# A two-layer decoder trunk: expert steps merged in pairs, their products chained in program order, and the last scale spread by rounded products

## The chip, the cores and the metric

The kernel runs on one core of one Trainium2 chip. The metric is the device time of one execution in microseconds; of before three runs are given, and their median counts. A profile is one further execution, taken by the hardware profiler.

## The reference, cut to what matters

The input is 256 tokens of 1024 values in float32. Two layers follow a first layer norm; each has a token mixer (two attention branches, not touched by this change apart from its first products) and a channel mixer: a dense SwiGLU in layer 0, and in layer 1 eight experts of which each token takes two.

```python
def moe_swiglu(x, w_router, w_gate_up, w_down):
    logits = (x @ w_router).astype(jnp.float32)
    top_v, top_i = lax.top_k(logits, TOP_K)
    gates = jax.nn.softmax(top_v, axis=-1)
    combine = jnp.sum(jax.nn.one_hot(top_i, N_EXPERTS, dtype=jnp.float32) * gates[..., None], axis=-2)
    y = jnp.zeros_like(x)
    for e in range(N_EXPERTS):
        y = y + combine[..., e:e + 1].astype(x.dtype) * swiglu(x, w_gate_up[e], w_down[e])
    return y

    # each sub-layer, in reference():
    h = layer_norm(DEEPNORM_ALPHA * h + f, ln_ffn_g[l], ln_ffn_b[l])
```

An expert has a gate-and-up matrix of 1024 x 7168 and a down matrix of 3584 x 1024, all float32: eight of them are 352 MB, and every one is read, whatever the router says.

## The kernel before, in words

The work stands in program order: first layer norm, mixer of layer 0, `out_norm` (residual and layer norm), the dense channel mixer, `out_norm`, mixer of layer 1, `out_norm` with the router beside it, and then the experts, which end in the last layer norm. A scheduler orders each engine's instructions by their priority (program order, apart from the parts under `high_priority`) and by dependencies that the kernel adds by hand. TensorE, VectorE (DVE), ScalarE (ACT) and the queue of DMA issues (SP) each work off their own list in order: an instruction that waits holds up all behind it on its engine.

**The experts.** The experts are put into eight places by how many tokens they have. Places 0, 1 and 2 form the *big* chain, places 7, 6, 5, 4 and 3 the *small* one. Each chain is a Python generator that gives one step at a time.

- A step of the big chain loads one piece of 1024 KB or less into a `raw` buffer (`slot`, L389). ACT makes its upper part `whi` (L433) and DVE the rest `wlo` (L434), in halves of 128x1024, and `tile_mm` multiplies them: eight products with the rounded tokens (`whi,xh` and `whi,xl`, alternating) and four `wlo,xh`, called *rounded products* below; they go to TensorE at L304. At place 0 a third set of tokens rides along, `far`: its products read the raw piece itself (`mm<-raw,xs`, 64 columns). They are collected in `beside` and issued for two steps together (`together`, called by `step`).
- A step of the small chain loads two pieces (768 KB in the up part, 1024 KB in the down part) and multiplies the raw float32 values with packed tokens (`aux<-raw,xs` in the up part, `aux<-raw,eh` in the down part; no split).

Both chains draw their `raw` buffers from one ring of eight (`RING`); a buffer comes free when the last instruction that reads it is done, and the next load into it waits on SP for that. The pieces of the first eight small steps are loaded ahead, seven of them in the ring and nine in a second pool (`AHEAD`, L382), and the ring also takes one piece of the ninth step ahead of its turn. The eight small steps go first. Then `both_chains` opens the pool for `whi` and calls `merge`, which takes one step of one chain or the other so that both get through the parts of `MERGE` in proportion:

```python
while i < ex or j < ey:
    if i < ex and (i - at[0]) * (ly - at[1]) <= (j - at[1]) * (ex - at[0]):
        i += 1
        yield next(x)
    else:
        j += 1
        yield next(y)
```

Inside a step, `in_turn` chains the products of a Packed tile one behind the other; those of `tile_mm` are not chained and not tied to what stands before or behind them. `later_on` puts a small function off to the end of a later step (`flush`): transposes, sums, and the spread below.

**The last scale.** `spread_rows` (called at step 160) loads the gain and the bias of the last layer norm, 1024 values each, as four rows of 512 (L1620) and spreads each over 128 partitions: one float32 product with a row of ones into a `tp` bank (two buffers), and a copy by ACT (L1613), all four in one put-off function.

**The first half.** `keep_busy` (L306) issues products of ones whose result nobody reads (`o<-onesb`). `out_norm` issues three of them at its end, for both tiles of 128 tokens alike, then the scale and the shift of tile 0 and of tile 1 (`ln_scale`: small DVE steps L491 and L495; L546: the shift with gain and bias), and after each tile its transposes (L469). The silu of the dense mixer is on ACT (L1071), with a product on DVE (L1072 before, L1075 after the change).

Of the kernel before, what the change touches and what calls it, by code (L numbers as in the profile page):

```python
# [9 lines left out]
F32R = mybir.dt.float32r  # L10
# [69 lines left out]
class Packed:  # L80
# [138 lines left out]
    def last(self, keys, ws, st):  # L219
# [9 lines left out]
        def products(x, ks, w, first, last):  # L229
            out = []  # L230
            for i, (r, _, j) in enumerate(ks):
                out += self.times([(x[half[i % 2]], 512 * i, 512)], self.hid[r, j], w, first and i < 2, last and i >= len(ks) - 2)
            b.in_turn(out, [w.load])

# [35 lines left out]
class Body:  # L270
# [463 lines left out]
    def mixer(self, l, xT):  # L734
# [7 lines left out]
        for i, k0 in enumerate((0, 2, 4, 6)):  # L742
            wpc = self.piece(w[:, k0:k0 + 2, C_FV:C_FV + 520], self.hold if i else self.first)
            for t in range(2):
                for hf in range(2):
                    if i == 0:
                        vps[t, hf] = self.aux_bank() if hf else self.mm_bank()
                    self.tok(vps[t, hf][:, :260], xT, k0, wpc, t, hf * 260, hf * 260 + 260, i == 0, i == 3)
        if l == 0:
            with tc.issue_after(self.made.ins):  # L750
                self.setup_bias()
# [158 lines left out]
        for i in range(2):  # L910
            wpc = [self.piece(wb[j][:, :, 512 * i:512 * i + 512]) for j in range(2)]
            for jp in range(2):
                parts = []
# [40 lines left out]
    def out_norm(self, h, xT, w, nk, g, b, routed=False):  # L954
# [26 lines left out]

        def norm(t):
            if t == 0:
                out.extend(self.stream("hT"))
            return self.ln_apply(r[t], self.ln_scale(st[t]), gb,
                                 lambda hf: self.put_T([out[0][p, hf] for p in "hl"], r[t][:, hf * 512:(hf + 1) * 512], t))
# [29 lines left out]
        with self.tc.manual_schedule(engines={mybir.EngineType.PE}):  # L1016
            for i in range(3):
                load(*p[i])
                go(*p[i], 0, 0)
                go(*p[i], 0, 1)  # L1020
            load(*p[3])
            for n, (i, part, t) in enumerate(((0, 0, 1), (0, 1, 1), (1, 0, 1), (3, 0, 0), (3, 1, 0), (1, 1, 1), (2, 0, 1), (2, 1, 1), (3, 0, 1), (3, 1, 1))):
                go(*p[i], t, part)
                for f, *x in behind.get(n, ()):
                    if routed and n == 9:
                        self.keep_busy(3, spare)
                    f(*x)
            self.keep_busy(11 if routed else 3, spare)
        if routed:
# [15 lines left out]
        with self.tc.high_priority():  # L1045
            self.hold = norm(0)
        self.first, self.late = None, self.hold
        norm(1)
        return r, out[1]

# [218 lines left out]
    def tile_mm(self, outs, x, w, flats, first, last):  # L1269

        for n, out in enumerate(outs):
            for i, act in enumerate(x):
                for j, part in ((0, "h"), (1, "h")):
                    self.mm(out, act[j], w.at(part, flats[i] + n * 512, 512), first and i + j == 0, False)
        for n, out in enumerate(outs):
            for i, act in enumerate(x):
                self.mm(out, act[0], w.at("l", flats[i] + n * 512, 512), False, last and i == len(x) - 1)

    def together(self, products=(), loads=()):

        products, loads = list(products), list(loads)
        for p, l in self.beside:
            products += p
            loads += l
        self.beside = []
        if products:
            self.in_turn(products, loads)

# [6 lines left out]
    def in_turn(self, products, after=()):  # L1295
# [7 lines left out]
        for x, y in zip(made, made[1:]):  # L1303
            self.behind(y, x, mybir.DependencyClass.NoSync)

    def behind(self, ins, other, kind):
# [167 lines left out]
    def moe(self, ctx, h, routing, g, b):  # L1474
# [19 lines left out]
        eidi = next(routing)  # L1494
        self.put_off, self.nrows = [], 5
        acc = []
# [31 lines left out]
        def merge(x, y, parts, lead):  # L1528
# [4 lines left out]
            for n, (ex, ey) in enumerate(ends):  # L1533
                ly = ey - (lead if n == len(ends) - 1 else 0)
                while i < ex or j < ey:
                    if i < ex and (i - at[0]) * (ly - at[1]) <= (j - at[1]) * (ex - at[0]):
                        i += 1
                        yield next(x)
                    else:
                        j += 1  # L1540
                        yield next(y)
                at = ex, ey
# [12 lines left out]
        for n, z in enumerate(both_chains()):  # L1555
# [17 lines left out]
            if n == 160:  # L1573
                gb = self.spread_rows(g, b)
            if n == 14:
# [23 lines left out]
    def spread_rows(self, g, b):  # L1599

        nc = self.nc
        one = self.wk.tile([1, 128], F32, name="one_row", bufs=1)
        nc.gpsimd.memset(one, 1.0)
        gb = [[self.pp.tile([128, 512], F32, name="ln_gb", tag="far", bufs=4) for _ in range(2)] for _ in range(2)]
        for row, xs in zip((g, b), gb):
            for hf, x in enumerate(xs):
                nc.sync.dma_start(x[0:1], row[None, hf * 512:(hf + 1) * 512])

        def f():
            for x in gb[0] + gb[1]:  # L1610
                bk = self.tp_bank()
                self.mm(bk, one, x[0:1], True, True)
                nc.scalar.activation(x, bk, AF.Copy)  # L1613
        self.later_on(f)
        return gb

# [155 lines left out]
```

## Time and profile before

| | us |
|---|---|
| median of three runs | 1463.91 (1463.39 to 1464.29) |
| the profiled execution | 1463.79 |
| its span in the profile | 1462.1 |
| TensorE busy | 1399.9 (96%) |
| DVE busy | 812.4 (56%) |
| ACT busy | 655.4 (45%) |

The busy time of TensorE (PE) is modelled to the end of a product, waits inside a pipelined row among it, so that 96% does not mean that it works at its peak; PEld is the weight load that runs beside it. The page cuts the span into 40 slices and gives for each the busy tenths of an engine, the TensorE clock that was granted (PEclk) and the share of the 16 DMA engines. The row DMA and the row GB/s are the ones to read beside the engines: 453.42 MB are moved, 310 GB/s over the span. An engine in square brackets in a timeline row is what ended its idle time.

### The profile page before, as it was taken

The page shows a single profiled execution, that of the slowest core. Times are in us where ns is not written, and L with a number is a line of the kernel's source. Part 1 is how long each engine was busy: PE and PEld are TensorE (multiplying, and loading weights), DVE is VectorE, ACT ScalarE, POOL GpSimd, SP SyncE. Part 2 cuts the span into 40 slices and gives each one's busy share as a digit, 9 for nine tenths or more (in the row PEclk, how much of TensorE's full clock was granted, in tenths as well). Part 3 has the DMA queues.
Part 4 walks back from the last instruction along what each step waited for, and adds up shares of the span by engine and source line. Part 5 has one row for each costly group of instructions (what it writes and reads, how often), then busy time and mean ns, then how long its engine had stood idle before and what let it go on. Part 6 is the DMA issues. An engine that isn't in the chain of part 4 may idle for free. (4 is left out here: it accounts for less than half of the span.)

```text
span 1462.1 us, 20101 instructions
## 1 busy us (share of the span) xinstructions
PE 1399.9 (96%) x7581; PEld 929.2 (64%) x7581; DVE 812.4 (56%) x1233; ACT 655.4 (45%) x954; POOL 16.9 (1%) x44
## 2 busy tenths in 40 slices
PE   8999999999999999999999999999999999999985
PEld 6878978888788789755444453467675455445531
DVE  7757786665577676624253443377667245344423
ACT  4656546664266663133433332356555233323310
POOL 4000000000000000000000000000000000000000
PEclk9999999999999999999999999999999899999998
DMA  9633546555384347699999999999999899999994
GB/s 297 220 120 135 181 146 205 198 167 207 106 265 151 115 145 300 253 385 407 405 418 415 415 419 422 420 419 418 418 420 420 331 421 409 421 420 420 419 366 189
DMA packets 135767, 453.42 MB, mean 310 GB/s; under 512 B 8079, under 2 KB 63399, under 8 KB 108013
## 3 DMA queue, kind: packets, MB, share of 16 engines
q1 hardware_dynamic: 134872, 450.99, 79.5%
q0 software_dynamic: 784, 1.05, 0.4%
q8 instruction: 62, 1.02, 0.3%
q14 instruction: 45, 0.36, 0.1%
q10 hardware_dynamic: 4, 0.01, 0.0%
HBM read 450.96 MB, written 1.05 MB: 309 GB/s over the span
## 5 line engine op out<-in xcount | busy, mean ns | idle before, releaser
L434 DVE TENSOR_TENSOR wlo<-raw,whi 128x1024 fp32r<-128x1024 f32 (+2 forms) x456 | 516.6, 1161 | 414.7 <-ACT whi L433 402.5
L433 ACT ACTIVATE whi<-raw 128x1024 fp32r<-128x1024 f32 (+2 forms) x456 | 442.1, 1005 | 380.9 <-DMA raw<-in_w_expert_gate_up 140.4
L304 PE MATMUL mm<-hT,whi 128*128 128x512 f32 x672 | 234.8, 398 | 0.0
L304 PE MATMUL aux<-raw,xs 128*32 128x512 f32 (+3 forms) x1280 | 188.1, 552 | 4.3 <-DMA raw<-in_w_expert_gate_up 3.5
L304 PE MATMUL mm<-hT,wlo 128*128 128x256 f32 x672 | 175.8, 281 | 0.0
L304 PE MATMUL mm<-whi,xh 128*128 128x512 f32 x336 | 140.7, 419 | 4.7 <-ACT whi L433 3.4
L304 PEld LDWEIGHTS mm<-hT,whi 128*128 128x128 f32 x672 | 121.5, 188 | 23.8 <-issue 0.7
L304 PE MATMUL mm<-whi,xl 128*128 128x512 f32 x336 | 133.2, 396 | 0.0
L304 PEld LDWEIGHTS mm<-hT,wlo 128*128 128x128 f32 x672 | 126.8, 189 | 9.1 <-issue 2.0
L304 PEld LDWEIGHTS aux<-raw,xs 128*32 128x32 f32 (+1 forms) x1280 | 57.4, 121 | 108.6 <-issue 99.4
L304 PE MATMUL aux<-raw,eh 128*32 128x512 f32 (+1 forms) x560 | 93.0, 604 | 11.3 <-DMA raw<-in_w_expert_down 7.7
L304 PE MATMUL mm<-wlo,xh 128*128 128x512 f32 x336 | 98.7, 402 | 0.8 <-DVE wlo L434 0.7
L304 PEld LDWEIGHTS mm<-whi,xh 128*128 128x128 f32 x336 | 63.4, 189 | 56.6 <-issue 23.2
L304 PE MATMUL mm<-whi,eh 128*128 128x512 f32 x336 | 89.1, 405 | 5.6 <-ACT whi L433 5.6
L304 PEld LDWEIGHTS mm<-whi,eh 128*128 128x128 f32 x336 | 59.7, 188 | 36.7 <-ACT whi L433 18.6
L304 PEld LDWEIGHTS mm<-wlo,xh 128*128 128x128 f32 x336 | 62.2, 189 | 23.1 <-DVE wlo L434 4.6
L304 PEld LDWEIGHTS mm<-whi,xl 128*128 128x128 f32 x336 | 63.5, 189 | 11.7
L304 PEld LDWEIGHTS aux<-raw,eh 128*32 128x32 f32 (+1 forms) x560 | 26.2, 121 | 60.7 <-issue 58.2
L429 ACT ACTIVATE sums<-mm 128x512 f32<-128x512 f32 x84 | 50.2, 600 | 31.9 <-PE mm L304 30.5
L304 PE MATMUL aux<-hT,whi 128*128 128x512 f32 x160 | 56.2, 396 | 0.0
L304 PE MATMUL mm<-raw,xs 128*64 128x512 f32 x224 | 54.2, 605 | 0.0
L304 PE MATMUL mm<-whi,hT 128*128 128x260 f32 (+2 forms) x192 | 50.9, 335 | 1.2 <-DVE hT L434 0.9
(345 smaller groups left out, 1607.8 us busy)
## 6 DMA issues: line engine op xcount, KB each, us to landing
raw<-in_w_expert_gate_up SPq DMA_DIRECT2D x140, 1024.0 KB, 11.9
raw<-in_w_expert_down SPq DMA_DIRECT2D x111, 1024.0 KB, 12.7
raw<-in_w_expert_gate_up SPq DMA_DIRECT2D x112, 768.0 KB, 11.5
raw<-in_w_in SPq DMA_DIRECT2D x36, 1024.0 KB, 5.1
raw<-in_w_ffn_gate_up SPq DMA_DIRECT2D x22, 1024.0 KB, 5.1
raw<-in_w_ffn_down SPq DMA_DIRECT2D x10, 1024.0 KB, 4.9
raw<-in_w_out SPq DMA_DIRECT2D x8, 1024.0 KB, 5.0
raw<-in_w_in SPq DMA_DIRECT2D x8, 520.0 KB, 6.7
```

The lines of the kernel that those rows point to most:

```text
L304: self.made = self.nc.tensor.matmul(out, lhsT, rhs, start=start, stop=stop)
L429: self.nc.scalar.activation(x, bank, AF.Copy, scale=scale)
L433: return (self.nc.scalar.activation(hi, src, AF.Copy), self.nc.vector.tensor_sub(lo, src, hi.bitcast(F32)))
L434: self.nc.vector.tensor_sub(lo, src, hi.bitcast(F32)))
```

## The change

It has five parts.

1. `merge` takes two steps of a chain at a time.
2. `in_line` chains a group's products like `in_turn`, and also ties its first product behind the last one of the group before (`self.line`), for both chains: on TensorE all products of expert pieces stand in program order. In `tile_mm` the products are the same, in the same order.
3. `spread_rows` splits each of the four rows into two rounded parts and spreads it by two rounded one-row products and an ACT copy, one row every fourth step from step 164 on.
4. `keep_busy` gets nine products in place of three in the two out_norms that have no router, and eight are added in the first mixer, among the products of its values.
5. The scale of the second tile in `out_norm` is computed at the high priority of the first tile's norm.

```diff
@@ first mixer
+                if l == 0 and i == 2 and t == 0:
+                    self.keep_busy(8, self.o_bank(), self.made)
@@ out_norm
-        def norm(t):
+        def norm(t, scale):
...
-            return self.ln_apply(r[t], self.ln_scale(st[t]), gb,
+            return self.ln_apply(r[t], scale, gb,
...
-            self.keep_busy(11 if routed else 3, spare)
+            self.keep_busy(11 if routed else 9, spare)
...
-            self.hold = norm(0)
+            self.hold = norm(0, self.ln_scale(st[0]))
+            scale = self.ln_scale(st[1])
...
-        norm(1)
+        norm(1, scale)
@@ tile_mm, together and Packed.last
+        self.in_line(products)
...
-            self.in_turn(products, loads)
+            self.in_line(products, loads)
@@
+    def in_line(self, products, after=()):
+
+        made = self.in_turn(products, after)
+        if self.line:
+            self.behind(made[0], self.line, mybir.DependencyClass.NoSync)
+        self.line = made[-1]
@@ merge
-                        i += 1
-                        yield next(x)
+                        for _ in range(min(2, ex - i)):
+                            i += 1
+                            yield next(x)
                     else:
-                        j += 1
-                        yield next(y)
+                        for _ in range(min(2, ey - j)):
+                            j += 1
+                            yield next(y)
@@ experts
             if n == 160:
-                gb = self.spread_rows(g, b)
+                gb, spreads = self.spread_rows(g, b)
+            if n > 160 and n % 4 == 0 and spreads:
+                self.later_on(spreads.pop(0))
@@ spread_rows
+        oner = self.wk.tile([1, 128], F32R, name="one_row_r", bufs=1)
+        nc.vector.tensor_copy(oner, one)
...
-        def f():
-            for x in gb[0] + gb[1]:
-                bk = self.tp_bank()
-                self.mm(bk, one, x[0:1], True, True)
-                nc.scalar.activation(x, bk, AF.Copy)
-        self.later_on(f)
-        return gb
+                def f(x=x):
+                    parts = [self.row_tile("parts", F32R)[0:1] for _ in range(2)]
+                    self.split(*parts, x[0:1])
+
+                    def spread():
+                        bk = self.tp_bank()
+                        self.in_turn([(bk, oner, p, i == 0, i == 1) for i, p in enumerate(parts)])
+                        nc.scalar.activation(x, bk, AF.Copy)
+                    self.later_on(spread)
+                spreads.append(f)
+        return gb, spreads
```

Three places of the order follow. The first is TensorE (PE) behind the eighth small step, before the change: the next two small steps (`aux`; `raw_6073` is the piece loaded ahead) stand ahead of the transposes of the eighth step's rows and of the first big piece, `raw_6265`, whose far product stands among its rounded products.

```order
L304 MATMUL aux_6299<-raw_6073,xs_6075 32x384 x4
L304 MATMUL aux_6299<-raw_6297,xs_6075 32x384 x4
L304 MATMUL aux_6299<-raw_6312,xs_6075 32x384 x4
L304 MATMUL aux_6299<-raw_6314,xs_6075 32x384 x4
L148 MATMUL tp_6290<-ident_123,rows_6250 128x128 x4
L304 MATMUL mm_6275<-whi_6267,xh_6139 128x512
L304 MATMUL mm_6275<-whi_6267,xl_6140 128x512
L304 MATMUL mm_6276<-whi_6267,xh_6139 128x512
L304 MATMUL mm_6276<-whi_6267,xl_6140 128x512
L304 MATMUL mm_6289<-raw_6265,xs_6141 64x512 x4
```

After the change the transposes come first, then 24 rounded products of two big pieces (the last six of them are shown), then the far products of both, `raw_6286` and `raw_6318`, and then the small steps, from the piece loaded ahead (`raw_6094`) on.

```order
L304 MATMUL mm_6297<-whi_6324,xh_6160 128x512
L304 MATMUL mm_6297<-whi_6324,xl_6161 128x512
L304 MATMUL mm_6296<-wlo_6321,xh_6160 128x512
L304 MATMUL mm_6296<-wlo_6325,xh_6160 128x512
L304 MATMUL mm_6297<-wlo_6321,xh_6160 128x512
L304 MATMUL mm_6297<-wlo_6325,xh_6160 128x512
L304 MATMUL mm_6310<-raw_6286,xs_6162 64x512 x4
L304 MATMUL mm_6310<-raw_6318,xs_6162 64x512 x4
L304 MATMUL aux_6350<-raw_6094,xs_6096 32x384 x4
L304 MATMUL aux_6350<-raw_6348,xs_6096 32x384 x4
L304 MATMUL aux_6350<-raw_6359,xs_6096 32x384 x4
```

So the two small steps have moved behind two big ones, and the far product that reads `raw_6286` last behind all rounded products of both.

The second place is SP's list of loads at the same place, with what each waits for. Before, the first big piece is followed by small ones and big ones in turn:

```order
L389 DMA raw_6265<-in_w_expert_gate_up 128x2x1024 [waits DMAHW7_49,PE_49]
L389 DMA raw_6297<-in_w_expert_gate_up 128x1536 [waits DMAHW0_49,PE_49]
L389 DMA raw_6312<-in_w_expert_gate_up 128x1536 [waits DMAHW1_49,PE_49]
L389 DMA raw_6314<-in_w_expert_gate_up 128x1536 [waits DMAHW2_49,PE_49]
L389 ISA
L389 DMA raw_6324<-in_w_expert_gate_up 128x2x1024 [waits DMAHW3_49,PE_49]
L389 DMA raw_6346<-in_w_expert_gate_up 128x1536 [waits DMAHW4_49,PE_49]
```

After it, two big pieces come first, then seven small ones, of which the sixth (`raw_6383`) is the first to wait for the buffer of the big piece `raw_6286`, which DVE and TensorE read:

```order
L389 DMA raw_6286<-in_w_expert_gate_up 128x2x1024 [waits DMAHW7_49,PE_49]
L389 ISA
L389 DMA raw_6318<-in_w_expert_gate_up 128x2x1024 [waits DMAHW0_49,PE_49]
L389 DMA raw_6348<-in_w_expert_gate_up 128x1536 [waits DMAHW1_49,PE_49]
L389 DMA raw_6359<-in_w_expert_gate_up 128x1536 [waits DMAHW2_49,PE_49]
L389 DMA raw_6361<-in_w_expert_gate_up 128x1536 [waits DMAHW3_49,PE_49]
L389 DMA raw_6371<-in_w_expert_gate_up 128x1536 [waits DMAHW4_49,PE_49]
L389 DMA raw_6373<-in_w_expert_gate_up 128x1536 [waits DMAHW5_49,PE_49]
L389 DMA raw_6383<-in_w_expert_gate_up 128x1536 [waits DMAHW6_49,DMAHW7_49,DVE_49,PE_49]
```

The second big piece is loaded before the small ones now, and the eighth load of the list has become dependent on TensorE's first far product.

The third place is DVE in the first `out_norm`, at the scale of the second tile. Before, the steps of the scale (L491, L495) and the shift (L546) stand ahead of the dense mixer's product with the silu:

```order
L495 SCALAR_TENSOR_TENSOR rs_y_2210<-rs_q_2211,rs_y_2210 128x1
L491 SCALAR_TENSOR_TENSOR rs_q_2211<-rs_y_2210,rs_m_2212 128x1
L495 SCALAR_TENSOR_TENSOR rs_y_2210<-rs_q_2211,rs_y_2210 128x1
L546 SCALAR_TENSOR_TENSOR h_2013<-h_2013,rs_y_2210,ln_gb_2008 128x512
L546 SCALAR_TENSOR_TENSOR h_2013<-h_2013,rs_y_2210,ln_gb_2010 128x512
L1072 TENSOR_TENSOR silu_2310<-silu_2310,mm_2261 128x256
```

After it, that product stands ahead of the last step of the scale:

```order
L495 SCALAR_TENSOR_TENSOR rs_y_2225<-rs_q_2226,rs_y_2225 128x1
L491 SCALAR_TENSOR_TENSOR rs_q_2226<-rs_y_2225,rs_m_2227 128x1
L1075 TENSOR_TENSOR silu_2325<-silu_2325,mm_2276 128x256
L495 SCALAR_TENSOR_TENSOR rs_y_2225<-rs_q_2226,rs_y_2225 128x1
L546 SCALAR_TENSOR_TENSOR h_2022<-h_2022,rs_y_2225,ln_gb_2017 128x512
L546 SCALAR_TENSOR_TENSOR h_2022<-h_2022,rs_y_2225,ln_gb_2019 128x512
```

The product of the silu has moved up by three rows, and the two L546 behind it.

More of the change, by code (lines that the diff above doesn't have):

```diff
@@ L232, in products @@
                 out += self.times([(x[half[i % 2]], 512 * i, 512)], self.hid[r, j], w, first and i < 2, last and i >= len(ks) - 2)
-            b.in_turn(out, [w.load])
+            b.in_line(out, [w.load])
         def give(h, t, y):
@@ L1269, in tile_mm @@
     def tile_mm(self, outs, x, w, flats, first, last):
+        products = []
         for n, out in enumerate(outs):
             for i, act in enumerate(x):
-                for j, part in ((0, "h"), (1, "h")):
-                    self.mm(out, act[j], w.at(part, flats[i] + n * 512, 512), first and i + j == 0, False)
+                for part in act:
+                    products.append((out, part, w.at("h", flats[i] + n * 512, 512), first and i == 0 and part is act[0], False))
         for n, out in enumerate(outs):
             for i, act in enumerate(x):
-                self.mm(out, act[0], w.at("l", flats[i] + n * 512, 512), False, last and i == len(x) - 1)
+                products.append((out, act[0], w.at("l", flats[i] + n * 512, 512), False, last and i == len(x) - 1))
+        self.in_line(products)
     def together(self, products=(), loads=()):
@@ L1304, in in_turn @@
             self.behind(y, x, mybir.DependencyClass.NoSync)
+        return made
+    def in_line(self, products, after=()):
[3 more added lines that the diff above has]
+        self.line = made[-1]
     def behind(self, ins, other, kind):
@@ L1494, in moe @@
         eidi = next(routing)
-        self.put_off, self.nrows = [], 5
+        self.put_off, self.nrows, self.line = [], 5, None
         acc = []
@@ L1603, in spread_rows @@
         nc.gpsimd.memset(one, 1.0)
+        oner = self.wk.tile([1, 128], F32R, name="one_row_r", bufs=1)
+        nc.vector.tensor_copy(oner, one)
         gb = [[self.pp.tile([128, 512], F32, name="ln_gb", tag="far", bufs=4) for _ in range(2)] for _ in range(2)]
+        spreads = []
         for row, xs in zip((g, b), gb):
```

## The prediction

> **What bounds the kernel now.** I read the page first, for its slices and its DMA issues, then the waits of the DMA queue, then windows and the timeline where the slices dip. Each slice is 36.55 us.
>
> ```profile
> span 1462.1 us, 20101 instructions
> PEclk9999999999999999999999999999999899999998
> DMA  9633546555384347699999999999999899999994
> GB/s 297 220 120 135 181 146 205 198 167 207 106 265 151 115 145 300 253 385 407 405 418 415 415 419 422 420 419 418 418 420 420 331 421 409 421 420 420 419 366 189
> ...
> raw<-in_w_expert_gate_up SPq DMA_DIRECT2D x140, 1024.0 KB, 11.9
> raw<-in_w_expert_gate_up SPq DMA_DIRECT2D x112, 768.0 KB, 11.5
> ```
>
> The kernel has two parts. Up to the 17th slice (some 620 us) the DMA row reads 3 to 9 and TensorE sets the time. From the 18th on it reads 9 at about 420 GB/s, so there the expert weights set it: a microsecond in which no piece is under way is a microsecond of the result, one saved on TensorE is worth nothing. One slice breaks this line, the 32nd (331 GB/s, PEclk 8). A 1024 KB piece (1.049 MB) takes 1.049/0.42 = 2.5 us, one of 768 KB 1.87 us.
>
> What holds the next piece back is a buffer, as the DMA queue's own waits say, of which this is the largest (us in total, times, longest):
>
> ```profile
> SPq L389 <- PE aux L304: 396.5, 180, 13.2
> ```
>
> Such a wait costs nothing while earlier pieces are still on the way. So what matters is when a reading product lets a buffer go, and that is the order on TensorE, which this change rewrites.
>
> **The change: the order of steps (largest cost).** At the start of the experts stage, windows first (us, then busy time of PE, PEld, DVE, ACT, POOL, then clock, DMA share, GB/s), then the timeline (start, duration, count; in brackets the idle time before and its releaser):
>
> ```profile
> 620.00:622.00 2.00, 2.00 (x17) 1.04 (x10) 0.00 (x0) 0.00 (x0) 0.00 (x0) 1.00 0.89 334
> 634.00:636.00 2.00, 2.00 (x28) 1.06 (x24) 1.23 (x2) 1.30 (x2) 0.00 (x0) 1.00 0.42 175
> 636.00:638.00 2.00, 2.00 (x22) 1.14 (x15) 2.00 (x3) 1.70 (x3) 0.00 (x0) 1.00 0.81 227
> ```
>
> ```profile
> 624.11 13.13 PE L304 MATMUL aux<-raw,xs 128*32 128x512 f32 x128
> 634.70 2.95 ACT L433 ACTIVATE whi<-raw 128x1024 fp32r<-128x1024 f32 x3 [3.61 <-PE aux L304]
> 634.77 0.69 DVE L135 TENSOR_TENSOR rows<-aux,gsilu 128x512 f32<-128x512 f32 x1 [9.93 <-PE aux L304]
> 635.38 4.62 DVE L434 TENSOR_TENSOR wlo<-raw,whi 128x1024 fp32r<-128x1024 f32 x4
> 638.78 1.94 PE L304 MATMUL mm<-raw,xs 128*64 128x512 f32 x8
> 642.61 0.39 PE L304 MATMUL mm<-whi,xh 128*128 128x512 f32 x1
> 645.50 1.50 PE L304 MATMUL aux<-raw,xs 128*32 128x384 f32 x16
> ```
>
> Before, TensorE does eight small steps and then two more, the first of which reads the 17th piece that was loaded ahead and frees its buffer near 636; DMA is short there for 2×0.58 + 2×0.19 = 1.5 us (0.42 and 0.81 of two 2 us windows). After, the order puts both first big pieces and their riding far products ahead of that small step. SP's order says what is loaded meanwhile: seven pieces, two of 1.049 and five of 0.786 MB, 6.03 MB, 14.4 us at 0.42 MB/us from about 620.2, so the queue is dry at about 634.7, as before. The eighth waits for the buffer of the first big piece. That is read last by its far product, which now stands behind all 24 rounded products. Time of it: the rows of the eighth step are there at 634.77+0.69 = 635.46, their four transposes take some 0.5, to 636.0. One big piece takes from 642.61 to 645.50, 2.89 us; two make 5.8, to 641.8 (the splits, from 634.70 on ACT at 2.95/3 = 0.98 and on DVE at 4.62/4 = 1.16 a half, end at 640.0 and just keep ahead). The far products take 1.94, to 643.7, and bytes flow again at about 644.0. The hole is 644.0−634.7 = 9.3 instead of 1.5 us: **+7.7**. Its ends: nothing, if another buffer is free in time; +9.5, if the two pieces come two microseconds slower because they wait for their splits.
>
> It should be one hole only. From the second round on, two big pieces and four small ones stand in turn: 2.10+3.15 = 5.24 MB, 12.5 us of DMA, against 5.8+1.9+1.5 = 9.2 us of products (two small steps being the 1.50 row), so TensorE catches up. The chaining itself issues nothing: 0. The same pieces are loaded, on the same queue.
>
> **The spread of the last scale (largest gain).** The 32nd slice, in windows, with the rows that stand in it:
>
> ```profile
> 1137.00:1140.00 3.00, 3.00 (x6) 1.15 (x4) 0.00 (x0) 0.00 (x0) 0.00 (x0) 0.50 1.02 423
> 1140.00:1143.00 3.00, 3.00 (x5) 1.00 (x4) 0.00 (x0) 0.60 (x1) 0.00 (x0) 0.50 0.79 330
> 1143.00:1146.00 3.00, 3.00 (x7) 1.03 (x8) 0.73 (x1) 2.30 (x3) 0.00 (x0) 0.50 0.32 134
> 1146.00:1149.00 3.00, 3.00 (x8) 0.71 (x6) 3.00 (x4) 2.08 (x3) 0.00 (x0) 0.50 0.01 5
> 1149.00:1152.00 3.00, 3.00 (x13) 1.33 (x10) 0.91 (x1) 0.00 (x0) 0.00 (x0) 0.84 0.86 284
> ```
>
> ```profile
> 1131.21 0.39 PE L304 MATMUL mm<-whi,xh 128*128 128x512 f32 x1
> 1131.44 0.39 PE L304 MATMUL mm<-whi,xl 128*128 128x512 f32 x1
> 1132.69 1.12 PE L304 MATMUL tp<-ln_gb,one_row 1*128 1x512 f32 x2
> ...
> 1138.44 2.07 PE L304 MATMUL tp<-ln_gb,one_row 1*128 1x512 f32 x2
> 1143.70 0.60 ACT L1613 ACTIVATE ln_gb<-tp 128x512 f32<-128x512 f32 x1 [2.56 <-PE tp L304]
> 1145.27 4.63 DVE L434 TENSOR_TENSOR wlo<-raw,whi 128x1024 fp32r<-128x1024 f32 x4 [10.61 <-ACT whi L433]
> ```
>
> The clock stands at half, the copies of the spread wait on ACT for the one-row products, the splits of the big pieces stand behind them, and DVE idles 10.61 us. No buffer is freed, and DMA loses 3×(0.21+0.68+0.99+0.14) = 6.1 us. After, there are eight rounded products at the 0.23 spacing of the quoted pair (1.8 us), two at a time among big products, and each copy has its ready product some steps ahead; the four one-row splits on ACT and on DVE are bounded by a full split (0.98 and 1.16) each and lie under DMA. So the whole hole goes: **−6.1**; at worst one piece's buffer waits for one such pair of splits, 2.1 back, −4. Next late is again DMA.
>
> [...]
>
> **First mixer.** The same dip stands at 22 to 28 us, behind an idle TensorE:
>
> ```profile
> 22.00:24.00 2.00, 1.21 (x9) 1.24 (x10) 1.28 (x2) 1.10 (x2) 0.00 (x0) 0.90 1.10 348
> 24.00:26.00 2.00, 2.00 (x11) 2.00 (x10) 1.52 (x7) 0.89 (x4) 0.79 (x2) 0.50 1.10 349
> 26.00:28.00 2.00, 2.00 (x14) 2.00 (x14) 1.25 (x3) 0.97 (x2) 1.36 (x3) 0.75 1.07 376
> ...
> 21.29 0.63 PE L477 MATMUL tp<-ident,h 128*128 128x128 f32 x4 [2.18 <-issue]
> ```
>
> It costs 2×(0.10+0.50+0.25) = 1.7 us of TensorE. The eight new filler products fall into the 2.18 us gap (8×0.22 = 1.8; the 0.22 from the three of the next fence, (0.82−0.39)/2, with 0.39 for the last). I take **−1.2**, since DMA is full there too (1.07 to 1.10) and may set part of it; ends −1.7 and 0.
>
> **The two out_norms.** Six more fillers each, and the second tile's scale earlier:
>
> ```profile
> 208.11 0.82 PE L304 MATMUL o<-onesb 128*128 128x512 bf16 x3
> 210.64 1.32 PE L469 MATMUL tp<-ident,h 128*128 128x128 f32 x8 [1.71 <-DVE h L546]
> 219.23 0.38 ACT L1071 ACTIVATE silu<-mm 128x256 f32<-128x256 f32 x1 [1.55 <-PE mm L304]
> 219.38 1.41 DVE L546 SCALAR_TENSOR_TENSOR h<-h,rs_y,ln_gb 128x512 f32<-128x512 f32 x2
> 220.28 1.29 PE L469 MATMUL tp<-ident,h 128*128 128x128 f32 x8 [1.08 <-DVE h L546]
> 220.71 0.41 DVE L1072 TENSOR_TENSOR silu<-silu,mm 128x256 f32<-128x256 f32 x1
> ...
> 402.42 1.04 PE L469 MATMUL tp<-ident,h 128*128 128x128 f32 x8
> 411.81 1.29 PE L469 MATMUL tp<-ident,h 128*128 128x128 f32 x8 [1.26 <-DVE h L546]
> ```
>
> In the first the fillers end at 208.11+9×0.22 = 210.1, ahead of 210.64: hidden. But on DVE the silu product now stands ahead of the last step of the scale and of L546. It needs ACT's silu, which ends at 219.61, and takes 0.41: L546 starts near 220.2 instead of 219.38, and the transposes that wait for it follow: **+0.8** (0 if PE's queue has other work, 1.1 if the step after the product is late too). In the second, transposes move 1.3 us back, but the later ones wait for DVE as they did (1.26): **0**, −0.3 to +1.3.
>
> **Sum.** 7.7−6.1−1.2+0.8 = +1.2. The profiled execution took 1463.79 us (1462.1 of span and 1.7 around it), 0.1 under the median of 1463.91, so 1463.79+1.2 = **1465.0**. About 0.2%, 2.9 us, is what a measurement of this kernel tells from no change: the sum lies inside, between 1461.0 and 1466.8.
>
> **Rivals.** *Faster: no hole opens at the start.* If the eighth piece gets its buffer by 636, as before, 7.7 us fall out: 1465.0−7.7 = 1457.3. For it: before lost 1.5 there only, with a ring as deep; against it: the far product's place. Chance 0.25.
>
> *Slower: in-line pairs open holes at the changes of expert.* There a gathering, its transposes and the first split of a new expert stand in TensorE's chained order; while the big pair waits, ready small pieces can't be read, so no buffer is freed. This decides from the point at which TensorE lies behind by more than the 12.5−9.2 = 3.3 us that a round gives it. At the four changes of the small chain and the two of the big one a 2.5 us piece each is lost: 6×2.5 = 15, 1465.0+15 = 1480.0. For it: L389 waits for `aux` up to 13.2 us already; against it: SP's pieces come in that same order. Chance 0.15.
>
> *Slower: the clock falls all the same.* If it was not the form of the one-row products that halved it, but something in that place which stays, the splits are late again: 1465.0+6.1 = 1471.1. For it: PE read 3.00 of 3.00 as it fell; against: the first one-row products (1132.69) stand ahead of the fall, and a pair of them takes 1.12 before it and 2.07 after it. Chance 0.08.
>
> That the change does not do what it says is excluded by the order.
>
> **How the numbers follow.** The forecast holds 0.52, with its own range 1461 to 1469 by the bounds of its terms. The whole range reaches down past the first rival with the low ends of the mixer and of both out_norms (−0.5−0.8−0.3 and a margin, 1455.5) and up past the third (1472.5), leaving out the second. Faster by over 0.2%: the first rival and a tenth of the forecast, 0.30. Slower: the other two and a quarter of the forecast, 0.36. Same: the rest, 0.34.
>
> **What would show it.** In the changed profile: DMA share near 0 from 635 to 644 and L389 released by `mm` at its end; no slice under 9 in PEclk at 1137 and no DVE gap of 10 us there; clock 1.00 at 24 us; L546 0.8 later after the first out_norm; DMA 9 in every slice between 645 and 1410. A second hole inside the stage, or none at 635, makes the prediction wrong.

## The result and the profile after

| | us |
|---|---|
| changed kernel, median of six runs | 1477.08 (1474.17 to 1477.76) |
| before, median of its six runs | 1462.19 (1459.13 to 1464.29) |
| ratio | 1.0106, 95% interval 1.0089 to 1.0123 |
| profiled execution after, its span | 1477.16, 1475.5 |

The change made the kernel 1.1% slower; the forecast was 1465.0 in a range up to 1472.5. It came out on the side of the second rival, which had a chance of 0.15 and a price of 1480.0.

The page of the changed kernel, span and slices (36.9 us each here):

```profile
span 1475.5 us, 20150 instructions
...
PEclk9999999999999999999999999999999999999998
DMA  9643555555384448679999999999999999999984
GB/s 299 215 141 115 174 177 190 181 182 185 115 262 138 136 150 344 239 292 410 389 416 403 366 381 420 421 418 419 418 420 420 384 420 417 420 420 420 418 362 195
```

The hole of the 32nd slice is mostly filled (384 in place of 331 GB/s), but the 18th fell from 385 to 292, and the 20th, 22nd, 23rd and 24th now read 389, 403, 366 and 381 where they read 405, 415, 415 and 419. Counted in bytes that were not moved between 620 and 1416 us, against a steady 420 GB/s, DMA is short by 16.0 us before and by 29.2 after: 13.2 of the 13.4 us between the two spans lie there.

The start of the experts stage after, windows and then TensorE's timeline:

```profile
634.00:636.00 2.00, 1.11 (x11) 0.41 (x4) 1.15 (x2) 1.23 (x2) 0.00 (x0) 1.00 0.42 172
636.00:638.00 2.00, 2.00 (x11) 1.68 (x11) 2.00 (x3) 2.00 (x3) 0.00 (x0) 1.00 0.02 9
640.00:642.00 2.00, 2.00 (x11) 1.36 (x11) 0.08 (x1) 0.00 (x0) 0.00 (x0) 1.00 0.00 0
644.00:646.00 2.00, 2.00 (x16) 0.57 (x16) 0.00 (x0) 0.00 (x0) 0.00 (x0) 1.00 0.53 141
```

```profile
640.85 1.09 PE L304 MATMUL mm<-wlo,xh 128*128 128x512 f32 x4
641.86 3.65 PE L304 MATMUL mm<-raw,xs 128*64 128x512 f32 x16
645.45 4.08 PE L304 MATMUL aux<-raw,xs 128*32 128x384 f32 x48
```

DMA stops at 634.8. The next load is issued at 643.84, when the first half of the 16 far records at 641.86 is done, and bytes flow fully again from some 645 on. In windows of one microsecond the hole sums to 10.05 us of DMA, against 1.53 before: +8.5.

The second loss is new: holes of 0.4 to 2.4 us near 710, 715, 811, 840, 871 and 1164, 8.7 us in all. Before had none of these above 0.25 us. Of the 13.2 us, 8.5+8.7−6.1 = 11.1 are named by this (6.1 being the hole of the spread, which is gone); the rest are dips too small to be counted as holes. The first of the new holes, in windows:

```profile
708.00:710.00 2.00, 2.00 (x11) 0.88 (x11) 0.00 (x0) 0.66 (x2) 0.00 (x0) 1.00 1.02 410
710.00:712.00 2.00, 2.00 (x12) 0.57 (x8) 0.00 (x0) 0.00 (x0) 0.00 (x0) 1.00 0.62 225
712.00:714.00 2.00, 2.00 (x20) 0.42 (x16) 0.00 (x0) 0.00 (x0) 0.00 (x0) 1.00 0.91 307
```

What stands behind it is seen in the DMA queue's issues (start, time from the first to the last of the group, count). Before, from 696 to 716 us:

```profile
696.34 0.39 SPq L389 DMA_DIRECT2D raw<-in_w_expert_gate_up  x1
697.20 2.23 SPq L389 DMA_DIRECT2D raw<-in_w_expert_down  x2
702.86 0.39 SPq L389 DMA_DIRECT2D raw<-in_w_expert_gate_up  x1
703.72 5.17 SPq L389 DMA_DIRECT2D raw<-in_w_expert_down  x2
```

After, in the same stretch:

```profile
690.50 3.92 SPq L389 DMA_DIRECT2D raw<-in_w_expert_down  x4
697.75 1.25 SPq L389 DMA_DIRECT2D raw<-in_w_expert_gate_up  x2
710.78 3.93 SPq L389 DMA_DIRECT2D raw<-in_w_expert_down  x4
```

The ring of eight is now refilled in bursts of six. Between the end of one burst (697.75+1.25 = 699.0) and the next issue (710.78) lie 11.8 us; before, the longest pause here was 4.5 (from 704.06 to 708.54, between the two issues of the last row). The waits of the queue say the same (us in total, times, longest); the line to read is that of the product `mm`, which lets the big pieces go. Before:

```profile
SPq L389 <- PE mm L304: 54.0, 42, 3.0
```

And after, where it held the queue three times as long, and at most 10.0 us:

```profile
SPq L389 <- PE aux L304: 226.3, 169, 6.9
SPq L389 <- DVE wlo L434: 210.9, 100, 10.4
SPq L389 <- PE mm L304: 163.3, 43, 10.0
```

And this is one such round of TensorE after, from the first rounded product of a pair to the next pair:

```profile
682.76 0.48 PE L304 MATMUL mm<-whi,xh 128*128 128x512 f32 x1
...
688.52 3.65 PE L304 MATMUL mm<-raw,xs 128*64 128x512 f32 x16
692.10 1.92 PE L304 MATMUL aux<-raw,eh 128*32 128x512 f32 x16
693.96 0.69 PE L148 MATMUL tp<-ident,rows 64*128 64x64 f32 x4
694.58 0.75 PE L1358 MATMUL tp<-ident,silu 128*128 128x128 f32 x4
695.16 1.52 PE L304 MATMUL tp<-hot,h 128*128 128x192 f32 x8
696.62 1.92 PE L304 MATMUL aux<-raw,eh 128*32 128x512 f32 x16
698.47 2.87 PE L304 MATMUL tp<-hot,h 128*128 128x192 f32 x16
```

Two big pieces take 688.52−682.76 = 5.8 us, their far products 3.65, four small pieces of the down part 2×1.92, the transposes 1.4: 14.7 us, for six pieces of 2.5, 15.0 us of DMA. The margin of this round is 0.3 us, and the gathering for the next expert (`tp<-hot,h`) puts 4.4 us more into it.

A small margin alone opens no hole, though. Before, a round of single steps in the up part has none at all:

```profile
672.05 1.94 PE L304 MATMUL mm<-raw,xs 128*64 128x512 f32 x8
676.91 1.50 PE L304 MATMUL aux<-raw,xs 128*32 128x384 f32 x16
678.33 1.94 PE L304 MATMUL mm<-raw,xs 128*64 128x512 f32 x8
```

From one far product to the next it is 678.33−672.05 = 6.28 us, for one big piece and two small ones, 2.5+2×1.87 = 6.24 us of DMA, and the same gathering stands at 692 to 702 without a hole. So what differs is when the buffers come free: singly before, and after in bursts.

Nor does every hole stand behind a gathering. There are three gatherings after 650 us (from 695, 860 and 1090 on); the holes near 710, 715 and 871, 3.7 us in all, follow the first two, and the third opens none. Ahead of the hole near 811 no gathering stands, but a pair that waited for its first split and then ran partly at half the clock:

```profile
802.26 0.50 PE L304 MATMUL mm<-whi,xh 128*128 128x512 f32 x1 [1.63 <-ACT whi L433]
...
810.07 3.65 PE L304 MATMUL mm<-raw,xs 128*64 128x512 f32 x16
```

```profile
804.00:808.00 4.00, 4.00 (x12) 3.11 (x11) 2.88 (x3) 1.05 (x2) 0.00 (x0) 0.57 1.02 415
808.00:812.00 4.00, 4.00 (x20) 2.17 (x20) 0.23 (x1) 1.32 (x2) 0.00 (x0) 1.00 0.75 301
```

Its two big pieces took 810.07−802.26 = 7.8 us, against 5.8 above. What opened the holes near 840 and 1164 is not shown.

### The profile page after: what moved, and what is told of

Read it like the earlier page. It is cut to its first block, busy times and chain, and to the rows that moved or that the text cites. A ratio compares the mean times of both kernels' runs of the same rounds, so it can differ in the third digit from the quotient of the medians.

```text
span 1475.5 us, 20150 instructions
## 1 busy us (share of the span) xinstructions
PE 1398.5 (95%) x7601; PEld 943.5 (64%) x7601; DVE 813.2 (55%) x1238; ACT 657.0 (45%) x958; POOL 17.0 (1%) x44
## 3 DMA queue, kind: packets, MB, share of 16 engines
q0 software_dynamic: 784, 1.05, 0.4%
q8 instruction: 62, 1.02, 0.3%
HBM read 450.96 MB, written 1.05 MB: 306 GB/s over the span
## 5 line engine op out<-in xcount | busy, mean ns | idle before, releaser
L434 DVE TENSOR_TENSOR wlo<-raw,whi 128x1024 fp32r<-128x1024 f32 (+2 forms) x456 | 514.2, 1161 | 374.7 <-ACT whi L433 370.7
L304 PE MATMUL aux<-raw,xs 128*32 128x512 f32 (+3 forms) x1280 | 182.7, 552 | 7.9 <-DMA raw<-in_w_expert_gate_up 7.6
L304 PE MATMUL mm<-whi,eh 128*128 128x512 f32 x336 | 92.1, 410 | 6.9 <-ACT whi L433 6.5
L304 PE MATMUL mm<-raw,xs 128*64 128x512 f32 x224 | 51.2, 598 | 0.0
```

The costliest lines, as they stand in the source:

```text
L304: self.made = self.nc.tensor.matmul(out, lhsT, rhs, start=start, stop=stop)
L434: self.nc.vector.tensor_sub(lo, src, hi.bitcast(F32)))
```

## The experiments

Theory of the pairs: two big pieces and their riding far products in a row keep their ring buffers so long that the loads under way run out, once at the start and then where a gathering falls into a round. Rival, theory of the tie: the forced program order on TensorE does it, whatever the step. A third question is what the new spread was worth. Each set ran on one chip with the kernel before beside it, whose executions lie between 1456.2 and 1466.2 us in all sets. DMA lost is the sum of (1−share) over windows of one microsecond in holes of more than 0.25 us; the last column holds the ratio to before with its 95% interval.

| run | start | 650–912 | 1135–1185 | median us | ratio |
|---|---|---|---|---|---|
| before, first profile | 1.5 | 0 | 6.1 | 1463.79 (one) | |
| before, second profile | 1.6 | 0 | 1.6 | 1457.78 (one) | |
| changed kernel | 10.1 | 6.4 | 2.4 | 1477.08 | 1.0106 (1.0089–1.0123) |
| changed, again | 9.9 | 5.2 | 2.6 | 1477.64 | 1.0128 (1.0106–1.0151) |
| single steps, tie | 6.0 | 0 | 0 | 1460.16 | 1.0008 (0.9997–1.0019) |
| pairs, no tie | 2.7 | 7.2 | 3.1 | 1473.68 | 1.0095 (1.0074–1.0117) |
| pairs, tie, two small first | 3.4 | 3.0 | 0 | 1462.83 | 1.0026 (1.0014–1.0037) |
| pairs, tie, four small first | 2.8 | 5.9 | 0.7 | 1469.72 | 1.0054 (1.0032–1.0075) |
| single, tie, two small first | 2.3 | 1.0 | 0 | 1457.31 | 0.9973 (0.9959–0.9988) |
| pairs, tie, far alone | 9.4 | 5.9 | 0 | 1473.16 | 1.0096 (1.0077–1.0114) |
| neither pairs nor tie | 1.6 | 0 | 0 | 1457.80 | 0.9987 (0.9973–1.0001) |
| before, seven buffers | 1.2 | 0 | 3.1 | 1465.43 | 1.0041 (1.0028–1.0054) |
| changed, seven buffers | 9.9 | 8.7 | 7.1 | 1493.44 | 1.0233 (1.0211–1.0255) |
| rounded spread alone | 1.5 | 0.3 | 0 | 1457.81 | 0.9991 (0.9979–1.0002) |
| float32 spread, apart | 1.6 | 0.4 | 0.3 | 1458.60 | 0.9994 (0.9980–1.0009) |
| spread and mixer alone | 1.6 | 0 | 0 | 1456.29 | 0.9977 (0.9967–0.9986) |

**Single steps, with the tie.**

```diff
-                        for _ in range(min(2, ex - i)):
-                            i += 1
-                            yield next(x)
+                        i += 1
+                        yield next(x)
...
-                        for _ in range(min(2, ey - j)):
-                            j += 1
-                            yield next(y)
+                        j += 1
+                        yield next(y)
```

> The changed kernel with its merge taken back to one step at a time; the tie between groups, the rounded spread and the edits of the first half stay. Theory of the pairs (two big pieces and their far products in a row keep ring buffers longer than the loads under way last, so DMA runs dry at the start and once per gathering): the start hole falls from 10 us to 3 to 5 (one big piece still stands ahead of the small step), the holes of 1 to 2.4 us between 700 and 880 us go, and the time is 14 to 17 us under the changed kernel, 2 to 5 under before. Rival, theory of the tie (it is the program order that is forced on TensorE, whatever the step): the holes between 700 and 880 stay, and the time is no more than 6 us under the changed kernel.

The holes between 650 and 912 are gone, and the ratio falls from 1.0106 and 1.0128 to 1.0008: the theory of the tie falls. The start hole is longer than the 3 to 5 us that were expected, and the time did not come out under before: one big piece still stands ahead of the small step. The windows of this run show its hole, 6.0 us in all:

```profile
633.00:635.00 2.00, 1.11 (x13) 0.61 (x6) 1.36 (x2) 1.06 (x1) 0.00 (x0) 1.00 0.41 169
635.00:637.00 2.00, 2.00 (x11) 1.64 (x10) 1.84 (x3) 1.82 (x3) 0.00 (x0) 1.00 0.01 3
637.00:639.00 2.00, 2.00 (x21) 0.83 (x19) 2.00 (x2) 0.67 (x1) 0.00 (x0) 1.00 0.00 0
639.00:641.00 2.00, 2.00 (x16) 0.48 (x8) 0.12 (x1) 0.00 (x0) 0.00 (x0) 1.00 0.57 104
```

Its longest wait of the queue for `mm` is 1.4 us, against 10.0 with pairs:

```profile
SPq L389 <- PE mm L304: 51.9, 42, 1.4
```

**Pairs without the tie.**

```diff
         made = self.in_turn(products, after)
-        if self.line:
-            self.behind(made[0], self.line, mybir.DependencyClass.NoSync)
         self.line = made[-1]
```

> The changed kernel without the tie between groups (each group is still chained within itself); pairs, rounded spread and the edits of the first half stay. Theory of the pairs: the order on TensorE puts two small steps ahead of the first big pair again, so the start hole falls to about 1.5 us (8.5 less than in the changed kernel), but the holes between 700 and 880 us stay: about 1468, 4 to 6 us over before. Theory of the tie: all holes go, 14 us or more under the changed kernel, 2 to 6 under before.

The holes between 650 and 912 stay, as the theory of the pairs has it. The start hole is 1.6 us, with 1.1 more at 640 to 646 (2.7 in the table), and yet the time is only some 2 to 5 us under the changed kernel by the two ratios of that one, not 8: small holes further on take part of it back.

**The rounded spread alone.**

```diff
-                gb = self.spread_rows(g, b)
+                gb, spreads = self.spread_rows(g, b)
+            if n > 160 and n % 4 == 0 and spreads:
+                self.later_on(spreads.pop(0))
```

(with the new `spread_rows`, into the kernel before)

> The kernel before with the rounded, spread-out spreading of the last scale alone. As the prediction had it (the one-row float32 products and their copies hold up ACT and so the buffers): the 6.1 us hole at 1140 goes, and the time is 4 to 6 us under before. Rival (the halved clock there fell on this place by chance, and the hole with it): 0 to 2 us under before, and the halved clock turns up in some other place.

The hole is gone, but the median gains only 0.4 us, and the ratio 1.3 us with an interval that holds no change. What it takes away are the long executions: its twelve lie between 1457.0 and 1459.5, while 8 of the 29 of before beside it lie above 1460, up to 1464.4.

**Pairs and tie, two small steps first.**

```diff
             self.pp = self.side(self.later, "parts")
-            yield from merge(big, small, MERGE, 8)
+            for _ in range(2):
+                yield next(small)
+            yield from merge(big, small, ((42, 45),) + MERGE[1:], 8)
```

> The changed kernel with two more small steps ahead of the first big pair (the merge then counts 45 in place of 47 in its first part); pairs and tie stay. Theory of the pairs: the start hole falls to 1 to 2 us, 8 less, and the holes at the gatherings stay where a gathering meets a big pair: about 8 us under the changed kernel, 5 over before. If the start hole does not come from the place of the first small step, nothing moves.

The start hole falls as told, with 2.1 us at 644 to 648 left. But more is gained than the start: 8 to 10 thousandths by the ratios, 12 to 15 us. The holes at 710 and 811 are not there; 3.0 us of holes stand at 897 to 903, behind the second gathering. At 710 this run shows full DMA with the same pair and the same gathering on TensorE:

```profile
710.00:712.00 2.00, 2.00 (x12) 1.17 (x12) 0.00 (x0) 0.38 (x1) 0.00 (x0) 1.00 1.01 406
```

That was not expected by either theory, and two runs further down follow it up.

**The changed kernel again.** No edit.

> The changed kernel once more, on the chip of the next three, so that they have it beside them. Both theories: 1.0 to 1.1% over before, and DMA holes at the same places as in its first profile (some 10 us from 635 on, 1 to 2.5 us each near 710, 810, 870 and 1165), since they come from the order and the ring; the halved clock turns up in other places than in the first profile if it falls by chance.

The holes are where they were, the halved clock is at 656, 762, 786, 803, 905, 929 and 1131 us; in the first profile at 657, 787, 804, 906, 930 and 1131. So the places of the clock, too, repeat nearly all in these two profiles.

**Far products alone.**

```diff
-        full = len(self.beside) > 1
+        full = len(self.beside) > 0
```

> The changed kernel with the far products of place 0 issued right behind each big piece and not for two pieces together; pairs, tie and all else stay. Theory that the pair keeps ring buffers too long: the first of the two buffers comes free some 5 us sooner (one piece of 2.9 and one far of 1.9), so the start hole falls by about 5 us and the holes at the gatherings, at most 2.4 us each, nearly go: 8 to 12 us under the changed kernel. Rival (TensorE is simply behind with its products): the same products take the same time, and no more than 2 us are gained.

The gain is 4.7 us by the two ratios, between the two expectations. The first hole shrinks from 9.9 to 7.1, but a second one of 2.3 follows at 644, so the start gains only half a microsecond; by the order, the big pair itself is what stands there. The holes between 650 and 912, which were nearly to go, stay (5.9 us); only the one near 1164 is gone. So the late far product is not what opens most of them.

**Neither pairs nor tie.** Both edits above together.

> The changed kernel with neither pairs nor tie: what is left of the change is the rounded spread and the edits of the first half, and inside tile_mm the chain of one step. If the loss is all in the merge: the start hole is 1.5 us as before, no hole at 1140, and the time is that of the rounded spread alone, 0 to 2 us under before. If the edits of the first half cost something, it lies above before.

The start hole is 1.6 us, there is no other, and the time is that of the rounded spread alone within the intervals. The loss is all in the pairs and the tie together.

**The kernel before, a second look.** No edit.

> The kernel before, unchanged, for a second profile. If the halved clock at 1136 to 1150 and the 6.1 us hole belong to the one-row products, both are there again. If the clock fell there by chance, it is found elsewhere, the hole at the spread is smaller by most of its size, and the time is nearer 1458 than 1464.

Both halves of the question get a partial yes. The windows of this profile:

```profile
1137.00:1140.00 3.00, 3.00 (x7) 1.04 (x6) 0.00 (x0) 0.94 (x2) 0.00 (x0) 0.87 1.03 429
1140.00:1143.00 3.00, 3.00 (x10) 0.83 (x11) 1.77 (x2) 3.00 (x5) 0.00 (x0) 0.56 0.73 306
1143.00:1146.00 3.00, 3.00 (x15) 1.21 (x12) 2.87 (x3) 1.04 (x2) 0.00 (x0) 1.00 0.73 232
```

The clock falls again behind the one-row products, but from 1139 to 1143 only and not from 1136 to 1150, and the hole is 1.6 us, not 6.1. The execution took 1457.78 us: 4.5 us of hole less, 6.0 us of time less.

**The float32 spread, apart.**

```diff
-        def f():
-            for x in gb[0] + gb[1]:
+        def spread(x):
+            def f():
                 bk = self.tp_bank()
                 self.mm(bk, one, x[0:1], True, True)
                 nc.scalar.activation(x, bk, AF.Copy)
-        self.later_on(f)
-        return gb
+            return f
+        return gb, [spread(x) for x in gb[0] + gb[1]]
```

> The kernel before with its four float32 one-row products as they are, but one every fourth step and not four in one place. If it is their form that brings the halved clock (one row of 128 fed, 1.12 us a pair), a halved window still turns up near them, and time is lost where the window holds up ACT: 0 to 2 us under before, with runs up to 1464 as before. If it is that four copies in a row stand on ACT behind them, the hole at 1140 goes as with the rounded spread: 1 to 3 us under before, and no run above 1460.

Inconclusive: three of the four products still stood between 1131 and 1137 us, only the fourth at 1192. The profile caught no halved clock and no hole, but its executions still reach 1465.2, as before's do.

**Before, and the changed kernel, with seven buffers.** The same edit in each:

```diff
-RING, AHEAD = 8, 9
+RING, AHEAD = 7, 9
```

> The kernel before with seven ring buffers in place of eight (the piece that was loaded ahead into the eighth comes in its turn). One piece less is 2 to 2.5 us of DMA less under way. Theory that a round of single steps needs fewer buffers than the ring has: 0 to 5 us more than before, small holes at the gatherings only. Rival (TensorE is the limit in the experts stage, not the ring): nothing moves.

> The changed kernel with seven ring buffers in place of eight. Theory that a pair of big steps holds its two buffers for a whole round of six pieces, so that the ring is just too small: every round that was short is now short by 2 to 2.5 us more, and rounds that just kept up open holes too, 15 to 40 us over the changed kernel, far more than one buffer costs the kernel before. Rival: no more than one buffer costs the kernel before.

One buffer costs the kernel before 0.41%, 6.0 us, a little over the expected 0 to 5, though its profile shows no hole in a new place. The piece that is no longer loaded ahead is 1.9 us of that (0.786 MB at 0.42 MB/us), in both kernels. The buffer costs the changed kernel 1.0233−1.0128, 1.05%, 15.3 us, at the low end of what was expected, and its holes from 650 on grow from 7.8 to 15.8 us. So a ring that is too small for a round of pairs is borne out by the size of the loss, but not in each hole: those near 711 and 815 grow by 0.9 and 1.5 us and not by 2 to 2.5, the one near 874 does not grow, and 4.5 us of the growth stand at 1161 to 1182, where this one profile had its clock at half just before (1152 to 1159).

**Four small steps first.** As with two above, with `range(4)` and `(42, 43)`.

> The changed kernel with four more small steps ahead of the first big pair, not two (43 counted in place of 47); pairs and tie stay. If the holes at the gatherings hang on where a gathering falls in a round of pairs whose margin is near zero: the start hole is closed as with two, but holes of 1 to 2.5 us at gatherings are back in part, and the time is between that of two steps first and the changed kernel, 5 to 12 us over before. If a closed start hole is all that it takes: as with two steps first, 3 to 5 us over before.

Holes are back, with the start hole nearly closed, and the time lies between the two. One of 1.6 us, from 904 on, follows a gathering (from 899 on). The largest, 2.7 us from 799 on, does not: it stands behind a clock at half from 793 to 797, and the gathering from 707 on opens no more than two of 0.3 near 725. So a gathering opens a hole in some rounds of pairs and not in others.

**Single steps with the tie, two small ones first.** Both edits above together.

> The changed kernel with single steps (merge as before) and two more small steps ahead of the first big one; the tie stays. If the tie costs nothing in itself: the start hole of single steps with the tie (6 us) falls to about 1.5, no other hole opens, and the time is that of single steps without tie, 1 to 3 us under before. If it costs something: the time stays at or above before.

0.9973: the tie costs nothing once the first big piece stands behind the small steps. Against the same order with pairs (1.0026, on another chip) that is 0.53%, 7.7 us, for the pairs alone.

**The two parts that paid.**

```diff
+                if l == 0 and i == 2 and t == 0:
+                    self.keep_busy(8, self.o_bank(), self.made)
```

(and the rounded spread, into the kernel before)

> The kernel before with the two parts of the change that paid in the traces: the rounded, spread-out spreading and the eight products in the first mixer; single steps, no tie, the out_norms as before. By the terms as measured (1.4 us from the mixer, 1.6 to 6 us from the hole at the spread, by how long the halved clock lasts there): 2 to 4 us under before, and 1 to 2 us under the rounded spread alone.

0.9977, an interval clear of 1, and 1.4 thousandths, 2.0 us, under the ratio of the rounded spread alone; that one is from another chip, and the two intervals overlap. This version beats both kernels; with the tie, single steps and two small ones first the ratio is as low.

## Why the prediction was wrong

**The start hole was right.** Forecast 634.7 to 644.0 and +7.7; measured 634.8 to some 645 and +8.5. The steps hold: the two big pieces end at 641.86 (641.8 was worked out), the next load is issued with the end of the first far product, at 643.84, and the run with two small steps first closes most of the hole. One figure landed by luck: 1.94 us were taken for the far products of both pieces, which take 3.65, but only the first of them has to be done for the buffer. The hole needs the tie as well as the pairs: without the tie it is 2.7 us.

**The step that failed** is the one behind it: "It should be one hole only. From the second round on [...] 9.2 us of products [...] so TensorE catches up." The products of a round were priced from the wrong rows. The far row of 1.94 us with 8 records is that of one big piece; two take 3.65. The row of 1.50 us with 16 records is one small step of the up part, two pieces, and not two steps; in the down part a step takes 1.92. And 1.4 us of transposes were left out. So the round shown above is 14.7 of 15.0 us and not 9.2 of 12.5, and the margin that was to close every lag is 0.3 us and not 3.3.

That margin is not the whole of it, since rounds of single steps (6.28 us for 6.24, above) have none either and open no holes. What was not asked at all is how many pieces are under way when a round ends: bursts of six from a ring of eight, with a pause of 11.8 us between them. That pairs are what costs is shown by the four combinations of pairs and tie and by the two runs with two small steps first (7.7 us); that it goes by way of the ring is borne out by the longest wait for `mm` (10.0 us, against 1.4 with single steps) and by the runs with seven buffers, but not hole by hole.

The second rival had the direction. Its price was 15 us for gatherings at six changes of expert; the new holes measure 8.7 us, of which 3.7 follow gatherings. Its cause was told as the tied order, and that part is wrong: at the gatherings the tie costs nothing, the pairs do it.

**The spread was mis-sized.** The −6.1 was read rightly from the profile, and that hole did go. But the profile had caught a long fall of the clock: in the second profile of before the same hole costs 1.6 us. Measured alone, the rounded spread gains 0.9 thousandths, 1.3 us, with an interval from 3.1 us of gain to 0.3 of loss. A term read from one execution had been taken for the kernel's. In the traces the fall is one window of about 3.4 us in one profile of before and four in the other. By the Trainium skill, "TensorE: Matmul & The Clock Gate", Part 1 (the HAM clock gate), the window over which activity is watched is free-running, so that the same kernel measures 6, 11 or 14 slow products at its start. No run here shows whether that sets the length in the middle of a kernel.

The third rival, that it was not the form of these products, is not borne out: of the four profiles with float32 one-row products three (the first and second of before, and that with seven buffers) have a halved clock within 10 us behind them, and none of the twelve with rounded ones has. The fourth, that of the float32 spread apart, has three of the four products in the same place and no fall. Why the clock falls while PE reads 3.00 of 3.00 is not shown.

**The first half was right in its terms, but one cost was missed.** The dip at 24 us is gone, and the first transposes of `out_norm` come at 209.21 in place of 210.64, −1.4 for −1.2. In the window and the timeline after:

```profile
24.00:26.00 2.00, 2.00 (x20) 2.00 (x19) 1.33 (x5) 1.76 (x3) 0.20 (x1) 1.00 1.10 351
```

```profile
209.21 1.32 PE L469 MATMUL tp<-ident,h 128*128 128x128 f32 x8 [0.42 <-DVE h L546]
...
217.79 0.38 ACT L1074 ACTIVATE silu<-mm 128x256 f32<-128x256 f32 x1 [1.54 <-PE mm L304]
218.20 0.42 DVE L1075 TENSOR_TENSOR silu<-silu,mm 128x256 f32<-128x256 f32 x1 [0.48 <-ACT silu L1074]
218.73 1.42 DVE L546 SCALAR_TENSOR_TENSOR h<-h,rs_y,ln_gb 128x512 f32<-128x512 f32 x2
219.63 1.66 PE L469 MATMUL tp<-ident,h 128*128 128x128 f32 x8 [1.88 <-DVE h L546]
```

From the first transposes to the second it is 10.42 us where it was 9.64, +0.8 as forecast, and by the way that was forecast: the silu, its product, L546, the transposes (idle 1.88 where 1.9 follows from 1.08+0.8). Then 0.9 us more are lost, a cost that the prediction did not have: behind these second transposes the clock falls to half, from 220.3 to 223.6.

```profile
220.00:224.00 4.00, 3.97 (x21) 3.47 (x20) 1.95 (x4) 1.58 (x3) 0.00 (x0) 0.57 0.99 330
```

The transposes take 1.66 us in place of 1.29, and the first product of the dense mixer behind them (`mm<-hT,whi`) starts at 224.32 where it was 224.03: 0.65 us of gain have become 0.29 of loss. Nine of the ten profiles with the new out_norms have this fall between 219 and 226 us, and none of the six others has one between 220 and 226. The tenth, that of single steps with the tie, keeps the gain: its second `out_norm` has its later transposes at 410.69, against 411.81 before and 411.91 in the changed kernel. So the first half, forecast at −0.4, brought nothing.

Open is why two small steps first make the pairs miss the first gathering; that a gathering opens a hole in some rounds only is shown, not which step decides. At 811 there is a hint: that profile has no halved clock there, while the six other profiles with pairs have one within 10 us ahead of their hole at 799 to 818.

## What to carry to other kernels

When steps are merged in larger groups, work out for each kind of round the products of all that stands in it against its loads, with rows of that kind, and look in each row at how many pieces its records stand for. Then count the pieces still under way when the group's buffers come free: with bursts of six from a ring of eight, a pause of 11.8 us emptied the queue. Single steps had no more margin, 6.28 us of products for 6.24 of loads, and lost nothing. And before a stall in one profile is booked as a gain, look at it in a second profile of the same kernel.

## What was not expected of the hardware

In the two profiles of the changed kernel the halved clock falls in the same six places of the experts stage within 1 us (the second has a seventh, at 762), each time for about 3.4 us or a multiple. In the two profiles of before only the place at the spread is common. The falls come with the pairs: between 640 and 1130 us all seven profiles with pairs have three or more, and the nine with single steps have none. In the first profile of the changed kernel TensorE had just stood idle ahead of four of the six: 2.46 and 1.96 us ahead of the one at 657, 3.07 and 1.68 ahead of 787, 1.63 ahead of 804 and 1.66 ahead of 930.

A fall cost DMA nothing in one stretch with pieces under way (share 1.01 to 1.02 in the changed kernel from 904 to 916 us, with the clock at 0.50 to 0.84), up to 6 us at the spread, where it held up the engine that frees buffers, and behind the one at 804 a hole of 2.0 us stands; how much of that is the clock's is not shown. One ring buffer of 1 MB was worth 6.0 us to a kernel that showed no new hole for want of it, 1.9 of them for the piece that was no longer loaded ahead.
